# The second FFN's way down: sums of weights made earlier, shared sums kept in PSUM, splits of tokens moved to one engine

## The chip, the cores and the metric

The kernel runs on one core of one Trainium2 chip. The metric is the device time of one launch in microseconds (us); the number given is the median of three runs.

## The reference

One inference step of a backbone with one layer: a half-step FFN, a token mixer (latent attention beside a two-way gated recurrence), a second half-step FFN, a last norm. The change touches the second FFN alone. There are 1152 tokens (1024 latent, 128 context), 1024 model columns and 2816 hidden columns.

```python
def swiglu(h, w1, w3, w2):
    return (jax.nn.silu(h @ w1) * (h @ w3)) @ w2

def trunk_layer(x, mod, cache, lb, norm_g, ffn1, ffn2, mixer_w):
    m = [mod[:, i][:, None, :] for i in range(N_MOD)]
    x = x + 0.5 * m[2] * swiglu(modulate(x, norm_g[0], m[0], m[1]), *ffn1)
    mix, ctx = token_mixer(modulate(x, norm_g[1], m[3], m[4]), cache, lb, *mixer_w)
    x = x + m[5] * mix
    x = x + 0.5 * m[8] * swiglu(modulate(x, norm_g[2], m[6], m[7]), *ffn2)
    return x, ctx
```

## The kernel before

Everything is float32. A float32 product is made of three matmuls, high by high, high by low and low by high, where ScalarE copies the high part of an operand (`wh`, `hh`, `xh`) and VectorE or GpSimd (POOL) subtracts it from the operand for the low part (`wl`, `hl`, `xl`). The names `fp`, `wp` and `dp` are pools of small tiles, of weight tiles and of DRAM. The tokens stand in four quarters of 288 columns; `PAIRS` puts them into two pairs of quarters.

The hidden columns are 22 tiles of 128. **The way up** (`h @ w1`, `h @ w3`) makes tiles 0 to 2 plainly (`plain_block`), and 3 to 21 by seven half products in place of eight, after Strassen and Winograd (`fast_block`, in the order `PRODUCTS = (1, 6, 7, 5, 2, 4, 3)`). Such products need sums of weights: `fast_ops` makes them, on POOL at L1716, their high part on ScalarE at L1720 and their low part on VectorE at L1721. The finished tile goes to DRAM (`hs`); from two tiles, `pair_sums` makes seven sums of tokens and stores them (`xd`).

**The way down** (`@ w2`) takes tiles 3 to 18 in eight pairs, which make three groups: `GROUPS = (3, 2), (7, 3), (13, 3)` holds the first tile of a group and its number of pairs. This is `down_fast`. A group has four sweeps (`down_sweep`), for m = 0 to 3, which stand for output tiles m and m + 4. A sweep runs the seven products, each for both pairs of quarters, so that a sweep of a three-pair group has 7 x 2 x 9 = 126 matmuls of 128x288.

`down_ops` makes the weights of a unit (one group and one m): four loads of w2 quarters (a11, a21, a22, a12), four POOL sums at L1826 (s1 = a21 + a22, s2 = s1 - a11, a11 - a21, a12 - s2), and for each product the high part at L1830 and the low part at L1831. `down_xs` loads the tokens' sums (`xr`, L1844) and splits them (L1854 on ScalarE, L1855 on POOL, or on VectorE for the second pair of a group); those of the next group are made in the third and fourth sweep of a group.

VectorE evicts each product from its PSUM bank (`d`) into the residual stream `x`, times the gate, by `add` at L1871. Products 1 and 6 feed several outputs: their sums over the groups stay in SBUF tiles `S` (named `su`, L1889). In the last group each finished shared sum gives three more adds, the "folds" (`x<-su`); from the second sweep on one fold is run behind each product, and what is left runs beside the first plain tiles.

After the groups, the plain tiles follow: `down_group` for f = 0 and 1 (matmuls at L473 to L475, eviction at L502), then `down_last` for 2, 19, 20 and 21. Their tokens are loaded (`load_h`) and split (`split_h`, L2021 and L2022 for f = 0 and 1 in two halves, one on VectorE and one on POOL) in the last sweep, and their weights by `load_w` (POOL at L247).

A scheduler sets the order of each engine's instructions from the order of the program's lines and their readiness, and pools of tiles decide when a tile may be filled again: three tiles of 384 columns in "hf", two in "raw", eight in the wide pool. All DMAs are put out by SP, in one order.

Of the kernel before, what the change touches and what calls it, by code (L numbers as in the profile page):

```python
# [9 lines left out]
F32 = mybir.dt.float32  # L10
# [4 lines left out]
ALU = mybir.AluOpType  # L15
# [78 lines left out]
class Trunk:  # L94
# [1696 lines left out]

    def down_ops(self, w2):

        nc = self.nc
        units = [(f, n, m) for f, n in GROUPS for m in range(KT // 2)]
        raws = [None, None]

        def load(u, i):
            f, n, m = units[u]
            if i:  # L1800
                t = self.wide("wr")[:, :1024].rearrange("p (v c) -> p v c", v=2)
            else:
                t = self.wp.tile([P, 2, 512], F32, tag="raw", bufs=2, name="raw")
            raws[i] = t[:, :, : n * P]
            for v, (j, h) in enumerate((((0, 0), (1, 0)), ((1, 1), (0, 1)))[i]):
                src = w2[f : f + 2 * n].rearrange("(k h) p o d -> h p k (o d)", h=2)[h]
                nc.sync.dma_start(raws[i][:, v].rearrange("p (k d) -> p k d", k=n), src[:, :, ts(4 * j + m, P)])

        load(0, 0)
        load(0, 1)  # L1810
        c = 0
        for u, (f, n, m) in enumerate(units):
            (a11, a21), (a22, a12) = [(t[:, 0], t[:, 1]) for t in raws]
# [4 lines left out]
            src = {1: a11, 6: s2, 7: a21, 5: s1, 2: a12, 4: a22, 3: a12}  # L1818
            pre = {
                6: ((s1, a21, a22, ALU.add), (s2, s1, a11, ALU.subtract)),  # L1820
                7: ((a21, a11, a21, ALU.subtract),),
                3: ((a12, a12, s2, ALU.subtract),),
            }
            for i in PRODUCTS:
                for o, x, y, op in pre.get(i, ()):
                    nc.gpsimd.tensor_tensor(o, x, y, op)  # L1826
                t = self.wp.tile([P, 2, 512], F32R, tag=("wh", "wl")[c % 2], bufs=3, name="wd")
                wh, wl = t[:, 0, : n * P], t[:, 1, : n * P]
                c += 1
                nc.scalar.copy(wh, src[i])  # L1830
                nc.vector.tensor_sub(wl, src[i], wh)  # L1831
                yield [w.rearrange("p (k d) -> p k d", k=n) for w in (wh, wl)]
# [28 lines left out]
    def down_sweep(self, g, m, X, ops, made, gm, S, after):  # L1861
# [11 lines left out]
        for i in PRODUCTS:  # L1873
            wh, wl = made.pop(0)
            for r, (q0, q1) in enumerate(PAIRS):
# [29 lines left out]
    def down_fast(self, w2, X, xg, ops, made, load_h, split_h, gm, nxt):  # L1905
# [5 lines left out]
        for g, (f, n) in enumerate(GROUPS):  # L1911
            new = {} if g else X
            last = g == len(GROUPS) - 1
            for m in range(KT // 2):
# [6 lines left out]
                def after():  # L1921
# [33 lines left out]
    def ffn_fast(self, l, gm, nxt):  # L1955
# [59 lines left out]
        def split_h(f, raw):  # L2015
            new = partial(self.tt, F32R) if f in (16, 17) and not l else split
            hh, hl = new(name="hh")[:, :T], new(name="hl")[:, :T]
            if isinstance(raw, list):
                for v in range(2):
                    c = ts(v, 2 * QW)  # L2020
                    nc.scalar.copy(hh[:, c], raw[v])  # L2021
                    (nc.gpsimd if v else nc.vector).tensor_sub(hl[:, c], raw[v], hh[:, c])  # L2022
# [7 lines left out]

        dops, dmade, X = (self.down_ops(w2) if l else None), [], {}
        xg = self.down_xs(0, X) if l else None
        for f in range(plain, NF):
# [3 lines left out]
            for n in range(7):  # L2037
# [178 lines left out]
```

## Time and profile before

| what | us |
|---|---|
| median of three runs | 2887.63 (2882.78 to 2887.94) |
| profiled execution, its own time | 2883.36 |
| its span in the profile | 2881.6 |
| TensorE (PE) busy | 2780.9 |
| VectorE (DVE) busy | 2038.8 |
| ScalarE (ACT) busy | 1327.9 |
| POOL busy | 948.6 |

The second FFN's plain tiles of the way up stand at about 2085 to 2150 us of the span, its fast tiles from there to about 2600, the three groups of the way down from about 2590 to 2781, and the plain tiles of the way down after that. PE is the engine of matmuls; PEld, its weight loads, runs beside it. A matmul count in a window is how much was done in it. A row of the timeline gives the start, the time, the engine, the line, the operation, and in brackets the idle time before it with what ended it.

### The profile page before, as it was taken

The page shows a single profiled execution, that of the slowest core. Times are in us where ns is not written, and L with a number is a line of the kernel's source. Part 1 is how long each engine was busy: PE and PEld are TensorE (multiplying, and loading weights), DVE is VectorE, ACT ScalarE, POOL GpSimd, SP SyncE. Part 2 cuts the span into 40 slices and gives each one's busy share as a digit, 9 for nine tenths or more (in the row PEclk, how much of TensorE's full clock was granted, in tenths as well). Part 3 has the DMA queues.
Part 4 walks back from the last instruction along what each step waited for, and adds up shares of the span by engine and source line. Part 5 has one row for each costly group of instructions (what it writes and reads, how often), then busy time and mean ns, then how long its engine had stood idle before and what let it go on. Part 6 is the DMA issues. An engine that isn't in the chain of part 4 may idle for free.

```text
span 2881.6 us, 55237 instructions
## 1 busy us (share of the span) xinstructions
PE 2780.9 (97%) x21138; PEld 2642.9 (92%) x21138; DVE 2038.8 (71%) x4435; ACT 1327.9 (46%) x2714; POOL 948.6 (33%) x947
## 2 busy tenths in 40 slices
PE   6999999999999999999999999989999999999998
PEld 5999999999999998988998777679999999999997
DVE  7677777577778777877355777755766665569885
ACT  6432323321166676766535787731642322334322
POOL 0132233354222122222144444442432222236540
PEclk9999999999999999999999999999999999999999
DMA  6643343653121111112512001263543333256321
GB/s 237 207 144 128 125 124 117 221 209 111 63 81 55 50 57 37 57 47 70 173 52 75 18 16 30 77 218 101 177 138 103 107 118 102 81 177 215 110 83 66
DMA packets 189801, 315.15 MB, mean 109 GB/s; under 512 B 21408, under 2 KB 113632, under 8 KB 189536
## 3 DMA queue, kind: packets, MB, share of 16 engines
q1 hardware_dynamic: 189536, 311.61, 33.2%
q8 instruction: 167, 2.74, 0.4%
q14 instruction: 98, 0.80, 0.1%
HBM read 234.38 MB, written 77.15 MB: 108 GB/s over the span
## 4 chain that ended last, share of the span: by engine, by line
PE 44%; DVE 12%; ACT 7%; issue 3%; DMA 3%; POOL 1%; SPq 0%; DVEq 0%; ACTq 0%; POOLq 0%
PE b L1746 14%; PE d L1884 4%; PE mm L473 4%; PE mm L474 3%; PE mm L475 3%; DMA g<-sgates 2%; PE dn L473 1%; PE dn L475 1%; PE dn L474 1%; PE mps L1411 1%; PE sps L1452 1%; PE lv L960 1%; DVE KE L997 1%; PE sps L1453 1%; PE sps L1454 1%
## 5 line engine op out<-in xcount | busy, mean ns | idle before, releaser
L1746 PE MATMUL b<-xo,wo 128*128 128x288 f32 x3552 | 482.0, 295 | 0.0
L1746 PEld LDWEIGHTS b<-xo,wo 128*128 128x128 f32 x3552 | 474.3, 188 | 0.0
L1746 PE MATMUL b<-bh,wo 128*128 128x288 f32 x1776 | 365.0, 295 | 1.9 <-ACT et L1756 1.9
L473 PE MATMUL mm<-xh,wh 128*128 128x384 f32 (+1 forms) x1008 | 352.5, 350 | 10.7 <-DVE sg L750 5.6
L474 PE MATMUL mm<-xl,wh 128*128 128x384 f32 (+1 forms) x1008 | 342.3, 340 | 0.0
L475 PE MATMUL mm<-xh,wl 128*128 128x384 f32 (+1 forms) x1008 | 341.7, 339 | 0.0
L1746 PEld LDWEIGHTS b<-bh,wo 128*128 128x128 f32 x1776 | 288.6, 188 | 2.1 <-ACT et L1756 2.1
L502 DVE SCALAR_TENSOR_TENSOR x<-dn,modt,x 128x256 f32<-128x256 f32 (+4 forms) x472 | 225.6, 499 | 87.0 <-PE dn L475 85.9
L1746 PE MATMUL b<-bl,wo 128*128 128x288 f32 x888 | 261.4, 294 | 0.0
L1720 ACT CAST wo<-raw 128x512 fp32r<-128x512 f32 x185 | 114.8, 622 | 220.5 <-issue 95.4
L473 PEld LDWEIGHTS mm<-xh,wh 128*128 128x128 f32 (+1 forms) x1008 | 189.8, 188 | 20.7 <-DVE sg L750 7.4
L474 PEld LDWEIGHTS mm<-xl,wh 128*128 128x128 f32 (+1 forms) x1008 | 189.7, 188 | 2.3 <-issue 0.7
L475 PEld LDWEIGHTS mm<-xh,wl 128*128 128x128 f32 (+1 forms) x1008 | 189.4, 188 | 1.0
L1884 PE MATMUL d<-xd,wd 128*128 128x288 f32 x1344 | 183.2, 299 | 6.6 <-DVE x L1871 4.7
L1884 PEld LDWEIGHTS d<-xd,wd 128*128 128x128 f32 x1344 | 181.6, 191 | 8.2 <-ACT wd L1830 4.2
L1721 DVE TENSOR_TENSOR wo<-raw,wo 128x512 fp32r<-128x512 f32 x185 | 127.4, 689 | 77.6 <-ACT wo L1720 75.8
L1716 POOL TENSOR_TENSOR ws<-raw 128x256 f32<-128x256 f32 x74 | 63.1, 873 | 328.5 <-DMA raw<-in_w 293.1
L318 DVE SCALAR_TENSOR_TENSOR junk<-wada,cb 128x512 bf16<-128x512 f32 x224 | 163.1, 728 | 9.7 <-DMA wada<-in_w_aT 8.9
L1461 POOL TENSOR_TENSOR ehl<-e,ehl 128x512 fp32r<-128x512 f32 x93 | 121.7, 1313 | 140.8 <-ACT ehl L1459 79.6
L1746 PEld LDWEIGHTS b<-bl,wo 128*128 128x128 f32 x888 | 167.0, 188 | 0.0
L247 POOL TENSOR_TENSOR wl<-raw,wh 128x1024 fp32r<-128x1024 f32 (+3 forms) x51 | 101.4, 1988 | 174.4 <-ACT wh L246 157.2
L1716 POOL TENSOR_TENSOR raw<-raw,ws 128x256 f32<-128x256 f32 x74 | 55.3, 768 | 285.1 <-issue 278.7
(433 smaller groups left out, 7175.3 us busy)
## 6 DMA issues: line engine op xcount, KB each, us to landing
raw<-in_w SPq DMA_DIRECT2D x148, 256.0 KB, 3.4
wada<-in_w_aT SPq DMA_DIRECT2D x112, 256.0 KB, 3.1
raw<-in_w SPq DMA_DIRECT2D x42, 512.0 KB, 3.9
raw<-in_w_in SPq DMA_DIRECT2D x41, 512.0 KB, 3.4
xr<-xd SPq DMA_DIRECT2D x56, 288.0 KB, 3.7
hr<-hs SPq DMA_DIRECT2D x26, 576.0 KB, 6.0
hb<-hd SPq DMA_DIRECT2D x44, 288.0 KB, 3.3
hs<-et SPq DMA_DIRECT2D x84, 144.0 KB, 2.0
```

What stands on the lines that cost most here:

```text
L247: pin((eng or self.nc.gpsimd).tensor_sub(wl, raw, wh))
L318: nc.vector.scalar_tensor_tensor(junk, ws[n % 2], 1.0, cs[s], ALU.mult, ALU.mult, accum_out=o)
L473: pin(nc.tensor.matmul(ps, wh, xh, start=start and i == 0, stop=False))
L474: pin(nc.tensor.matmul(ps, wh, xl, start=False, stop=False))
L475: pin(nc.tensor.matmul(ps, wl, xh, start=False, stop=stop and i == n - 1))
L502: nc.vector.scalar_tensor_tensor(self.x[m][:, a:b], ps[:, a - lo : b - lo], self.modt[:, gm, m, s : s + 1], self.x[m][:, a:b], ALU.mult, A ...
L1461: eng.tensor_sub(el, e, eh)
L1716: nc.gpsimd.tensor_tensor(o[:, c], x[:, c], y[:, c], op)
L1720: nc.scalar.copy(wh, src[i])
L1721: nc.vector.tensor_sub(wl, src[i], wh)
L1746: nc.tensor.matmul(ps, w[:, k], x[:, k, :QW], start=first, stop=last, skip_group_check=home != i)
L1884: nc.tensor.matmul(ps, w[:, k], xv, start=start, stop=stop, skip_group_check=home != i)
```

## The change

A new generator, `pair_weights`, goes through the five pairs of the first two groups and the four m, 20 units in all. Each unit loads four 128x128 pieces of w2 into two tiles of the "hf" pool (L1802 and L1804 of the changed kernel), makes the four sums on POOL (L1807 to L1810), and stores the results to DRAM (`wsum`, L1812 and L1813). It has four steps a unit, and the fast blocks of the way up take one step behind every product but the fourth. `down_ops` then loads seven ready operands for a unit of the first two groups: those of products 1, 5 and 3 into "hf" tiles (`wq`, L1840), of 6 and 7 into a "raw" tile, of 2 and 4 into a wide tile; the units of the last group load four operands and make their sums on POOL as before (L1878).

In the last group the shared sum of product 6 is written back into its PSUM bank (L1944), and the folds read it from there; they run behind products 7, 5, 2, 4 and 3 of each of the four sweeps (1, 2, 1, 1 and 1 of them), so none is left after the last. In the last sweep the tokens of the first two plain tiles are loaded and split one product sooner or so, and both halves of a split are on POOL (L2075).

```diff
+    def pair_weights(self, w2):
+        nc = self.nc
+        self.wsum = self.dp.tile([sum(n for _, n in GROUPS[:-1]), P, KT // 2, 4, P], F32, name="wsum")
+        for j in range(sum(n for _, n in GROUPS[:-1])):
+            f = GROUPS[0][0] + 2 * j
+            for m in range(KT // 2):
+                a, b = [self.fp.tile([P, CW], F32, tag="hf", bufs=self.hfb, name="wq") for _ in range(2)]
+                (a11, a21, s1), (s2, a12, a22) = [[t[:, ts(i, P)] for i in range(3)] for t in (a, b)]
+                for v, o in enumerate((a11, a21)):
+                    nc.sync.dma_start(o, w2[f][:, 0, ts(4 * v + m, P)])
+                for v, o in enumerate((a12, a22)):
+                    nc.sync.dma_start(o, w2[f + 1][:, 0, ts(4 * v + m, P)])
+                yield
+                yield
+                nc.gpsimd.tensor_tensor(s1, a21, a22, ALU.add)
+                nc.gpsimd.tensor_tensor(s2, s1, a11, ALU.subtract)
+                nc.gpsimd.tensor_tensor(a21, a11, a21, ALU.subtract)
+                nc.gpsimd.tensor_tensor(a12, a12, s2, ALU.subtract)
+                yield
+                nc.sync.dma_start(self.wsum[j][:, m, 0:2], a[:, P:].rearrange("p (k d) -> p k d", k=2))
+                nc.sync.dma_start(self.wsum[j][:, m, 2:4], b[:, : 2 * P].rearrange("p (k d) -> p k d", k=2))
+                yield
...
     def down_ops(self, w2):
...
-            if u + 1 < len(units):
-                load(u + 1, 0)
-                load(u + 1, 1)
-            s1, s2 = [self.fp.tile([P, CW], F32, tag="hf", bufs=self.hfb, name="ws")[:, : n * P] for _ in range(2)]
...
+        units = [(j, n, m) for j, n in enumerate(n for _, n in GROUPS) for m in range(KT // 2)]
+        nxt = {}
+        def rows_of(f, n, h, c):
+            return w2[f : f + 2 * n].rearrange("(k h) p o d -> h p k (o d)", h=2)[h][:, :, ts(c, P)]
+        def load(u, key):
+            if u == len(units):
+                return
+            g, n, m = units[u]
+            j, f = sum(v for _, v in GROUPS[:g]), GROUPS[g][0]
+            own = g == len(GROUPS) - 1
+            part = lambda t, h: t[:, : h * n * P].rearrange("p (h k d) -> p h k d", h=h, k=n)
+            if key in (1, 5, 3):
+                if own:
+                    return
+                t = part(self.fp.tile([P, CW], F32, tag="hf", bufs=self.hfb, name="wq"), 1)[:, 0]
+                if key == 1:
+                    src = rows_of(f, n, 0, m)
+                else:
+                    src = self.wsum[j : j + n][:, :, m, {5: 1, 3: 3}[key]].rearrange("k p d -> p k d")
+                nc.sync.dma_start(t, src)
+                nxt[u, key] = t
+            elif key == 6:
+                t = part(self.wp.tile([P, 1024], F32, tag="raw", bufs=2, name="raw"), 2)
+                for v, kind in enumerate((2, 0)):
+                    src = rows_of(f, n, 0, 4 * v + m)
+                    if not own:
+                        src = self.wsum[j : j + n][:, :, m, kind].rearrange("k p d -> p k d")
+                    nc.sync.dma_start(t[:, v], src)
+                nxt[u, 6], nxt[u, 7] = t[:, 0], t[:, 1]
             else:
+                t = part(self.wide("wr"), 2)
+                for v in range(2):
+                    nc.sync.dma_start(t[:, v], rows_of(f, n, 1, 4 * v + m))
+                nxt[u, 2], nxt[u, 4] = t[:, 0], t[:, 1]
+        for key in (1, 6, 5, 2, 3):
+            load(0, key)
+        for u, (g, n, m) in enumerate(units):
+            load(u + 1, 6)
+            load(u + 1, 2)
+            if g == len(GROUPS) - 1:
+                a11, a21, a12, a22 = [nxt[u, i] for i in (6, 7, 2, 4)]
+                s1, s2 = [
+                    self.fp.tile([P, CW], F32, tag="hf", bufs=self.hfb, name="ws").rearrange("p (k d) -> p k d", k=n)
+                    for _ in range(2)
+                ]
+                pre = {
+                    6: ((s1, a21, a22, ALU.add), (s2, s1, a11, ALU.subtract)),
+                    7: ((a21, a11, a21, ALU.subtract),),
+                    3: ((a12, a12, s2, ALU.subtract),),
+                }
+                nxt.update({(u, 1): a11, (u, 6): s2, (u, 5): s1, (u, 3): a12})
+            else:
+                pre = {}
             for i in PRODUCTS:
...
+                src = nxt.pop((u, i))
+                wh, wl = [t[:, v, : n * P].rearrange("p (k d) -> p k d", k=n) for v in range(2)]
+                nc.scalar.copy(wh, src)
+                nc.vector.tensor_sub(wl, src, wh)
+                if i in (1, 5, 3):
+                    load(u + 1, i)
+                yield wh, wl
...
                 if i == 1 and first:
                     nc.scalar.copy(u, ps)
                 elif i in (1, 6):
-                    nc.vector.tensor_add(u, ps, u)
+                    nc.vector.tensor_add(ps if i == 6 and last else u, ps, u)
                     if i == 6 and last:
-                        self.folds += [partial(add, mi, q, u) for mi, q in ((m + 4, q1), (m + 4, q0), (m, q1))]
+                        self.folds += [partial(add, mi, q, ps) for mi, q in ((m + 4, q1), (m + 4, q0), (m, q1))]
                 elif i in (7, 5):
                     add(m + 4, q1, ps)
                 elif i == 2:
...
                         for _ in range(GROUPS[g + 1][1]):
                             next(xg, None)
                     elif last:
-                        if m:
+                        for _ in range((0, 0, 1, 2, 1, 1, 1)[k]):
                             self.folds.pop(0)()
                         if m == KT // 2 - 1:
-                            if k in (0, 3):
-                                raws.append(load_h(k // 3))
-                            elif k in (2, 4):
+                            if k in (0, 2):
+                                raws.append(load_h(k // 2))
+                            if k in (1, 3):
                                 pend.append(split_h(*raws.pop(0)))
-                            if k in (1, 5):
-                                ws.append(self.load_w(w2[k // 4], 1, D, home=partial(self.tt, F32R)))
+                            if k in (0, 2):
+                                ws.append(self.load_w(w2[k // 2], 1, D, home=partial(self.tt, F32R)))
                     elif not g and not m:
                         next(xg, None)
                     k += 1
...
         for f in rest[:2]:
             pend.append(split_h(*load_h(f)))
         fs, hs = zip(*pend[:2])
-        self.bg = (f() for f in self.folds)
+        assert not self.folds
         self.down_group(w2, fs, hs, gm, ws)
-        for _ in self.bg:
-            pass
         for f in rest[2:]:
             pend.append(split_h(*load_h(f)))
         fs, hs = zip(*pend[2:])
...
                 for v in range(2):
                     c = ts(v, 2 * QW)
                     nc.scalar.copy(hh[:, c], raw[v])
-                    (nc.gpsimd if v else nc.vector).tensor_sub(hl[:, c], raw[v], hh[:, c])
+                    nc.gpsimd.tensor_sub(hl[:, c], raw[v], hh[:, c])
                 return f, (hh, hl)
             nc.scalar.copy(hh, raw)
             nc.gpsimd.tensor_sub(hl, raw, hh)
...
         def load_w2(f):
             return self.load_w(w2[f], 1, D, home=spare if f % 2 else None)
 
+        sums = self.pair_weights(w2) if l else iter(())
         dops, dmade, X = (self.down_ops(w2) if l else None), [], {}
         xg = self.down_xs(0, X) if l else None
         for f in range(plain, NF):
...
                     g.send(w)
                     if n in ((1, 4) if l else (0, 1, 2, 4)):
                         next(ada, None)
+                if n != 3:
+                    next(sums, None)
                 if f == NF - 1 and l:
                     if n:
                         dmade.append(next(dops))
...
                     elif n == 5:
                         ws.append(load_w2(1))
                         self.x = [load_x(0), load_x(1)]
-        assert next(ada, 1) == 1
+        assert next(ada, 1) == 1 and next(sums, 1) == 1
         for t in self.puts:
             self.put(*t)
         if not l:
```

On POOL, in the plain tiles of the way up: `wl` is the low part of a weight of tile f = 1 or 2, `bl` the low part of tokens, whose matmuls follow. Before:

```order
L247 TENSOR_TENSOR wl_24499<-raw_24496,wh_24498 128x1024
L424 TENSOR_TENSOR bl_23433<-xn_24259,bh_23432 128x288
L424 TENSOR_TENSOR bl_23433<-xn_24278,bh_23432 128x288
L424 TENSOR_TENSOR bl_23433<-xn_24298,bh_23432 128x288
L424 TENSOR_TENSOR bl_23433<-xn_24317,bh_23432 128x288
L424 TENSOR_TENSOR bl_23435<-xn_24337,bh_23434 128x288
L424 TENSOR_TENSOR bl_23435<-xn_24356,bh_23434 128x288
```

The same place after the change, where `wq` are the two tiles of a unit of `pair_weights`:

```order
L247 TENSOR_TENSOR wl_24499<-raw_24496,wh_24498 128x1024
L1807 TENSOR_TENSOR wq_25172<-wq_25172,wq_25173 128x128
L1808 TENSOR_TENSOR wq_25173<-wq_25172 128x128
L1809 TENSOR_TENSOR wq_25172<-wq_25172 128x128
L1810 TENSOR_TENSOR wq_25173<-wq_25173 128x128
L424 TENSOR_TENSOR bl_23433<-xn_24259,bh_23432 128x288
L424 TENSOR_TENSOR bl_23433<-xn_24278,bh_23432 128x288
L424 TENSOR_TENSOR bl_23433<-xn_24298,bh_23432 128x288
L424 TENSOR_TENSOR bl_23433<-xn_24317,bh_23432 128x288
L424 TENSOR_TENSOR bl_23435<-xn_24337,bh_23434 128x288
L1807 TENSOR_TENSOR wq_25364<-wq_25364,wq_25365 128x128
L1808 TENSOR_TENSOR wq_25365<-wq_25364 128x128
```

The first unit's four sums now stand ahead of the subtractions of a token tile, and the second unit's among those of the next.

On SP, at the same place (`in_w13` and `in_w2` are weights in DRAM, `hs1` the finished tile, `hd1` the tokens' stage). Before:

```order
L252 DMA raw_24834<-in_w13 128x1024
L1637 DMA hs1_24209<-sl_24257 128x288
L419 DMA hd1_23440<-xn_24259 128x288
L419 DMA hd1_23440<-xn_24278 128x288
L419 DMA hd1_23440<-xn_24298 128x288
```

After:

```order
L1802 DMA wq_25172<-in_w2 128x128 x2
L1804 DMA wq_25173<-in_w2 128x128 x2
L252 DMA raw_24834<-in_w13 128x1024
L1802 DMA wq_25364<-in_w2 128x128
L1637 DMA hs1_24209<-sl_24257 128x288
L419 DMA hd1_23440<-xn_24259 128x288
L419 DMA hd1_23440<-xn_24278 128x288
L1812 DMA wsum_25171<-wq_25172 128x256
L1813 DMA wsum_25171<-wq_25173 128x256
L1802 DMA wq_25364<-in_w2 128x128
L419 DMA hd1_23440<-xn_24298 128x288
```

The unit's loads stand ahead of a weight load of the way up, and its stores, which follow POOL's sums, ahead of the stores of tokens.

On VectorE, in the last sweep of the last group (`d` are PSUM banks, `x` the residual stream, `modt` the gate, `su` a shared sum in SBUF). Before:

```order
L1871 SCALAR_TENSOR_TENSOR x7_29908<-d7_32040,modt_92,x7_29908 128x288
L1871 SCALAR_TENSOR_TENSOR x7_29908<-d7_32051,modt_92,x7_29908 128x288
L1871 SCALAR_TENSOR_TENSOR x7_29908<-d5_32069,modt_92,x7_29908 128x288
L1871 SCALAR_TENSOR_TENSOR x7_29908<-su_29912,modt_92,x7_29908 128x288
L1871 SCALAR_TENSOR_TENSOR x7_29908<-d5_32080,modt_92,x7_29908 128x288
L1871 SCALAR_TENSOR_TENSOR x7_29908<-su_29913,modt_92,x7_29908 128x288
L1871 SCALAR_TENSOR_TENSOR x3_29906<-d1_31980,modt_92,x3_29906 128x160
```

After:

```order
L1944 TENSOR_TENSOR d6_32261<-d6_32261,su_30158 128x288
L1944 TENSOR_TENSOR d6_32272<-d6_32272,su_30159 128x288
L1926 SCALAR_TENSOR_TENSOR x7_30154<-d7_32289,modt_92,x7_30154 128x288
L1926 SCALAR_TENSOR_TENSOR x7_30154<-d6_32261,modt_92,x7_30154 128x288
L1926 SCALAR_TENSOR_TENSOR x7_30154<-d6_32261,modt_92,x7_30154 128x160
L1926 SCALAR_TENSOR_TENSOR x7_30154<-d7_32300,modt_92,x7_30154 128x288
L1926 SCALAR_TENSOR_TENSOR x7_30154<-d6_32261,modt_92,x7_30154 128x128
L1926 SCALAR_TENSOR_TENSOR x3_30152<-d6_32261,modt_92,x3_30152 128x288
```

The shared sum is written into the bank `d6`, and the folds that read `su` before read that bank now, sooner behind product 6.

More of the change, by code (lines that the diff above doesn't have):

```diff
@@ L1792, in down_ops @@
     def down_ops(self, w2):
         nc = self.nc
[L1795 to L1801, printed above, removed]
-            else:
[L1803 to L1807, printed above, removed]
@@ L1809, in down_ops @@
-        load(0, 0)
-        load(0, 1)
-        c = 0
-        for u, (f, n, m) in enumerate(units):
-            (a11, a21), (a22, a12) = [(t[:, 0], t[:, 1]) for t in raws]
-            if u + 1 < len(units):
-                load(u + 1, 0)
-                load(u + 1, 1)
-            s1, s2 = [self.fp.tile([P, CW], F32, tag="hf", bufs=self.hfb, name="ws")[:, : n * P] for _ in range(2)]
[L1818 to L1823, printed above, removed]
+        units = [(j, n, m) for j, n in enumerate(n for _, n in GROUPS) for m in range(KT // 2)]
@@ L1826, in down_ops @@
                     nc.gpsimd.tensor_tensor(o, x, y, op)
+                src = nxt.pop((u, i))
                 t = self.wp.tile([P, 2, 512], F32R, tag=("wh", "wl")[c % 2], bufs=3, name="wd")
-                wh, wl = t[:, 0, : n * P], t[:, 1, : n * P]
+                wh, wl = [t[:, v, : n * P].rearrange("p (k d) -> p k d", k=n) for v in range(2)]
                 c += 1
-                nc.scalar.copy(wh, src[i])
-                nc.vector.tensor_sub(wl, src[i], wh)
-                yield [w.rearrange("p (k d) -> p k d", k=n) for w in (wh, wl)]
+                nc.scalar.copy(wh, src)
[3 more added lines that the diff above has]
+                yield wh, wl
     def down_xs(self, g, X):
```

## The prediction

> **What bounds the kernel now.** I read the page's head and chain first.
>
> ```profile
> span 2881.6 us, 55237 instructions
> PE 2780.9 (97%) x21138; PEld 2642.9 (92%) x21138; DVE 2038.8 (71%) x4435; ACT 1327.9 (46%) x2714; POOL 948.6 (33%) x947
> PE 44%; DVE 12%; ACT 7%; issue 3%; DMA 3%; POOL 1%; SPq 0%; DVEq 0%; ACTq 0%; POOLq 0%
> ```
>
> TensorE is busy 97% of the span and holds most of the chain. The change leaves the number of matmuls as it is, so it can only win what TensorE loses in stalls or at a lower clock, or add such losses. Where these are in the second FFN is seen by counting matmuls in the windows: length, PE busy (count), PEld, DVE, ACT, POOL, granted clock, DMA share, GB/s.
>
> ```profile
> 2105.00:2110.00 5.00, 3.63 (x16) 2.70 (x15) 3.68 (x9) 4.77 (x12) 2.91 (x4) 0.82 0.38 132
> 2140.00:2145.00 5.00, 2.98 (x23) 2.75 (x22) 5.00 (x8) 1.50 (x3) 3.75 (x5) 1.00 0.43 122
> 2200.00:2300.00 100.00, 100.00 (x759) 100.00 (x758) 68.18 (x145) 30.44 (x60) 29.34 (x37) 1.00 0.36 119
> 2620.00:2630.00 10.00, 8.76 (x66) 8.53 (x65) 9.48 (x20) 3.62 (x9) 5.63 (x6) 1.00 0.47 141
> 2630.00:2640.00 10.00, 7.93 (x57) 7.32 (x55) 9.24 (x15) 8.14 (x16) 7.87 (x6) 1.00 0.42 120
> 2640.00:2650.00 10.00, 9.34 (x59) 9.37 (x60) 9.28 (x16) 3.77 (x7) 10.00 (x7) 0.83 0.75 217
> 2660.00:2670.00 10.00, 10.00 (x78) 10.00 (x77) 7.47 (x14) 2.06 (x4) 2.21 (x3) 1.00 0.16 42
> 2710.00:2720.00 10.00, 9.05 (x67) 8.61 (x65) 7.97 (x11) 5.35 (x9) 10.00 (x7) 1.00 0.86 255
> 2720.00:2730.00 10.00, 8.34 (x51) 8.37 (x52) 9.96 (x19) 2.78 (x6) 6.24 (x5) 0.83 0.46 139
> 2780.00:2790.00 10.00, 5.15 (x23) 4.13 (x21) 9.89 (x8) 5.48 (x6) 10.00 (x5) 0.87 0.16 53
> 2790.00:2800.00 10.00, 9.43 (x45) 9.33 (x45) 5.57 (x13) 0.01 (x1) 4.71 (x2) 0.79 0.01 2
> 2800.00:2810.00 10.00, 10.00 (x59) 10.00 (x58) 6.46 (x14) 0.00 (x0) 0.00 (x0) 1.00 0.00 0
> ```
>
> An undisturbed stretch of the way down has 78 matmuls in 10 us (2660), one of plain tiles 59 (2800). The way up (2200 to 2300) never stops. So the losses stand at four joints:
>
> - J1, first to second group (2620 to 2650): 66 + 57 + 59 = 182 of 234; 52 missing at 7.8 per us are 6.7 us.
> - J2, second to last group (2710 to 2730): 118 of 156, 4.9 us.
> - J3, last group to the plain tiles (2780 to 2800): 23 + 45 = 68 of 118; 50 at 5.9 per us are 8.5 us.
> - J0, the plain tiles of the way up (2105, 2140): short stalls while VectorE prepares the tokens' sums.
>
> J1 to J3 together are 20.1 us, which is all that can be won there. Next, what ends the waits, from the timeline (start, us, engine, line, then idle time and its releaser).
>
> ```profile
> 2622.91 11.15 PEld L1884 LDWEIGHTS d<-xd,wd 128*128 128x128 f32 x84 [1.47 <-DVE x L1871]
> 2720.56 0.51 ACT L1830 CAST wd<-wr 128x384 fp32r<-128x384 f32 x1 [1.27 <-POOL wr L1826]
> 2721.63 13.49 PEld L1884 LDWEIGHTS d<-xd,wd 128*128 128x128 f32 x90 [2.07 <-ACT wd L1830]
> ...
> 2766.90 3.18 POOL L2022 TENSOR_TENSOR hl<-hr,hh 128x576 fp32r<-128x576 f32 x2 [2.91 <-ACT hh L2021]
> 2770.04 2.91 POOL L247 TENSOR_TENSOR wxl<-raw,wxh 128x1024 fp32r<-128x1024 f32 x1
> 2778.06 3.97 DVE L1871 SCALAR_TENSOR_TENSOR x<-su,modt,x 128x160 f32<-128x160 f32 x2
> 2784.21 2.83 POOL L2025 TENSOR_TENSOR hl<-hr,hh 128x1152 fp32r<-128x1152 f32 x1
> 2784.49 0.51 DVE L1871 SCALAR_TENSOR_TENSOR x<-d,modt,x 128x288 f32<-128x288 f32 x1
> 2785.03 2.32 DVE L1871 SCALAR_TENSOR_TENSOR x<-su,modt,x 128x288 f32<-128x288 f32 x1
> 2787.84 0.29 PEld L473 LDWEIGHTS dn<-hh,wxh 128*128 128x128 f32 x1 [4.34 <-DVE x L1871]
> ```
>
> J1 waits for VectorE's evictions, J2 for a weight sum of POOL, and J3 4.34 us for VectorE, whose adds of shared sums from SBUF (su) take 2 to 2.3 us each while POOL runs its long subtractions. The eviction from PSUM (d) at 2784.49, beside the same POOL instruction, takes 0.51.
>
> **J3: shared sums from PSUM, splits on POOL.** Durations by shape:
>
> ```profile
> L1871 DVE SCALAR_TENSOR_TENSOR x<-d,modt,x 128x288 f32<-128x288 f32 x96 | 47.0, 507 | 5.8 <-PE d L1884 5.4
> L1871 DVE SCALAR_TENSOR_TENSOR x<-su,modt,x 128x288 f32<-128x288 f32 x20 | 19.6, 979 | 0.4
> ```
>
> After the change all of these adds read PSUM (d6 in the order): 0.51 us instead of a mean of 0.98, and not 2 or more beside POOL. VectorE also gives up two halves of the first plain tiles' splits. None of the folds is left after the last sweep. VectorE should then be a product behind at 2781, not 6 us. POOL gains two halves of 3.18 / 2 = 1.6 us; its work of this stretch has idle time around it (2.91 before the first half), and by the row at 2770.04 its last weight split ended at 2773, so with 3.2 more it ends near 2776, ahead of the first plain matmuls at about 2781. The banks of product 6 now stay taken until their folds are done: the second pair's is written again 27 matmuls into the next sweep, 3.5 us at 7.8 per us, against folds of 0.5. In the first sweep of the last group six folds stand where none stood (+3 us of VectorE); that goes to J2. J3's bounds: 4 (only the 4.34 us wait goes, the half clock behind it stays) to 8.5. I take **−7.5**, near the upper end, because nothing of what VectorE does there still reads two SBUF operands.
>
> **J1 and J2: ready sums are loaded.** POOL loses four sums for each of the eight units of the first two groups:
>
> ```profile
> L1826 POOL TENSOR_TENSOR wr<-wr,ws 128x256 f32<-128x256 f32 x4 | 3.0, 741 | 11.4 <-DVE wd L1831 11.4
> L1826 POOL TENSOR_TENSOR ws<-raw,wr 128x256 f32<-128x256 f32 x4 | 4.0, 1008 | 0.0
> L1826 POOL TENSOR_TENSOR ws<-raw,wr 128x384 f32<-128x384 f32 x8 | 8.6, 1078 | 24.7 <-DMA wr<-in_w 22.7 <-issue 1.9
> L1826 POOL TENSOR_TENSOR raw<-raw 128x384 f32<-128x384 f32 x8 | 9.6, 1201 | 0.5
> ```
>
> That is 16 × 0.74 to 1.01 and 16 × 1.08 to 1.20, about 32 us less. At J1 POOL was busy up to 10.00 of 10 and VectorE 9.3; POOL gets room, and VectorE's subtractions run beside it less often. Against this stand seven loads a unit where four were, all in SP's one row; the three into the small ring are put out only after VectorE's low part (L1831) of the product before has freed their tile, and the token loads (xr) stand behind them. A load lands in some 3.6 us:
>
> ```profile
> wr<-in_w SPq DMA_DIRECT2D x8, 128.0 KB, 3.6
> ```
>
> One unit's lead covers that (126 matmuls of a three-pair unit are 16 us). J1's bounds: +2 (the new loads hold the xr loads for half a landing) to −6.7; I take **−3.5**, half the loss, since VectorE's evictions, which ended the wait, keep their own number and length. J2 waits for a sum of the last group's own unit, which stays on POOL and in the same place, but gets a less loaded POOL ahead of it and six more folds on VectorE: between +2.5 and −4.9, I take **−0.5**.
>
> [...]
>
> **J0 and the way up: the sums' new place.** POOL gets 80 adds of 128x128. The trace has none; between 0.40 (128x48) and the 0.74 above, by columns, 0.53 each, 2.1 a unit, 42 us in all.
>
> ```profile
> L907 POOL TENSOR_TENSOR Y<-fs,Y 128x48 f32<-128x48 f32 x72 | 28.5, 396 | 109.1 <-ACT Y L905 105.5
> 2097.43 1.57 POOL L424 TENSOR_TENSOR bl<-xn,bh 128x288 fp32r<-128x288 f32 x2 [0.35 <-ACT bh L423]
> PEld ps L474 <- POOL bl L424: 1.9, 4, 0.6
> 2115.10 5.46 DVE L1633 TENSOR_TENSOR xo<-hd,xo 128x288 fp32r<-128x288 f32 x4
> 2127.97 1.56 DVE L1633 TENSOR_TENSOR xo<-hd,xo 128x288 fp32r<-128x288 f32 x4
> ```
>
> On 42 us of an engine that is 29% busy in the way up, the average is harmless. But the order puts the first units into the plain tiles: the first four adds stand ahead of the bl subtractions at 2097, for which TensorE waits already, and the next four among them. One unit on that path is +2.1. VectorE's four subtractions took 5.46 us beside 4.8 us of POOL and 1.56 alone: 0.8 us lost for each us of POOL. Where VectorE is full (5.00 of 5 at 2140) another unit's 2.1 us thus cost 1.7. J0: **+3.8**, from 0 (the adds fall into POOL's idle time) to 6 (all three units on the path).
>
> [...]
>
> In the fast blocks the weights stand ready early:
>
> ```profile
> 2316.88 1.25 DVE L1721 TENSOR_TENSOR wo<-ws,wo 128x512 fp32r<-128x512 f32 x1 [3.05 <-ACT wo L1720]
> 2329.23 0.46 DVE L1750 TENSOR_TENSOR et<-b,et 128x288 f32<-128x288 f32 x1
> POOL ws L1716 <- DMA raw<-in_w: 159.1, 17, 11.7
> ```
>
> This low part is there at 2318.1, and its product, 12 matmuls ahead of its first eviction, starts at about 2327.6: 9.5 us of cover, against 2.1 of adds in front of a sum. I take **+0.5** (0 to 21, see below). If the cover were gone, each unit would cost its 2.1.
>
> **Sum.** −7.5 − 3.5 − 0.5 + 3.8 + 0.5 = −7.2. The profiled execution took 2883.36 us, 4.27 below the median of the runs (2887.63): 2876.2 on its scale, **2880.4** against the median. About 0.2%, 5.8 us, is what a measurement of this kernel can tell from no change: faster means below 2881.9, slower above 2893.4.
>
> **Rivals.**
>
> - *The loads take the sums' place* (chance 0.14). J1 and J2 keep their losses because TensorE waits for loads that SP holds back where it waited for VectorE and POOL. For: SP is in order, and the DMA share at J1 is 0.75 already. Against: the stretches have gaps at 0.42 to 0.47. −7.5 + 3.8 + 0.5 = −3.2, 2884.4.
> - *Slower: the way up is coupled to the pair sums* (0.16). SP holds a store of sums until POOL has made them; POOL makes them behind its own weight sums, which wait for raw loads (17 waits, 159.1 us), and those stand behind the store on SP. From the point where a raw load comes 9.5 us later than now, TensorE stops in the middle of a tile. Such a stop is taken at 3 us (1.5 idle, as at 2622.91, and 1.7 at the clock of 0.83 over 10 us). 80 steps, six a tile, run over 13 tiles; in half of them, 7 × 3 = 21: +13.8, 2901.4. For: the waits are up to 11.7 us already. Against: TensorE doesn't stop once from 2200 to 2300.
> - *J1 and J2 vanish and J0 is free* (0.10). −7.5 − 6.7 − 4.9 are −19.1, 2868.5. For: POOL's 10.00 of 10 at both joints. Against: VectorE's evictions remain.
> - *J3 doesn't go as said* (0.06): TensorE then waits for POOL, which now has all of the splits. Only 3 of 8.5 won: −2.7, 2884.9. For: POOL is 10.00 busy from 2780; against: its margin of 5 us above.
> [...]
>
> **How the numbers follow.** The forecast has 0.50. Of it 0.40 lie below 2881.9, since the J0 and J1 terms can each be off by 3; 0.10 within. Faster: 0.40 + 0.10 + 0.02 = 0.52. Within 0.2%: 0.10 + 0.12 + 0.05 + 0.02 = 0.29. Slower: 0.16 and the tails of the first and fourth rival, 0.03, are 0.19. The range begins at the third rival, 2868, and ends at 2895, where the forecast's costs all stand at their bad ends (−4 + 2 + 2.5 + 6 + 0.5 = +7); only the second rival lies outside.
>
> **What would show it.** Right: at J3 over 100 matmuls in the two windows, the folds at 0.5 us and no wait for VectorE above 1 us; at J1 POOL well below 10.00 and 25 matmuls more; in the plain tiles TensorE waits for bl by 2 us more; 2200 to 2300 with 759 matmuls still. Wrong: stops in the fast blocks released by wo or by raw loads, J3's wait handed to POOL's hl, or J0 longer by over 6 us.

## The result

The changed kernel takes 2880.3 us (median of 22 runs), the kernel before 2884.45 us in the 22 runs beside them: a ratio of 0.9985, 95% interval 0.9979 to 0.9992, so some 2 to 6 us less, 4.3 by the ratio. Forecast were 7.2 less, which lies outside this interval. The time itself, 2880.4 forecast and 2880.3 measured, agrees better than the difference only because the kernel before took 2884.45 us here and not the 2887.63 from which the forecast reckons; that is luck. The profiled executions have spans of 2881.6 and 2876.7 us.

The windows of the changed kernel (length, PE busy with its count, PEld, DVE, ACT, POOL, granted clock, DMA share, GB/s), at the four joints and in the way up:

```profile
2105.00:2110.00 5.00, 3.18 (x16) 2.27 (x16) 3.17 (x8) 4.49 (x11) 3.99 (x7) 1.00 0.67 218
2200.00:2300.00 100.00, 100.00 (x759) 100.00 (x758) 68.32 (x144) 28.12 (x60) 42.81 (x62) 1.00 0.47 151
2620.00:2630.00 10.00, 9.63 (x73) 9.38 (x72) 7.64 (x20) 3.48 (x8) 2.99 (x2) 1.00 0.83 262
2630.00:2640.00 10.00, 7.92 (x59) 7.55 (x58) 6.62 (x12) 6.95 (x14) 4.92 (x4) 1.00 0.66 197
2640.00:2650.00 10.00, 6.21 (x36) 6.00 (x35) 10.00 (x14) 4.81 (x9) 8.76 (x5) 0.83 0.79 233
2710.00:2720.00 10.00, 10.00 (x78) 10.00 (x77) 8.99 (x13) 5.39 (x9) 10.00 (x7) 1.00 0.81 254
2720.00:2730.00 10.00, 7.73 (x57) 7.32 (x56) 8.57 (x16) 4.61 (x9) 7.09 (x6) 1.00 0.69 207
2730.00:2740.00 10.00, 9.40 (x71) 9.17 (x70) 9.83 (x25) 2.06 (x4) 4.27 (x4) 1.00 0.19 52
2780.00:2790.00 10.00, 10.00 (x67) 10.00 (x66) 6.45 (x15) 5.36 (x6) 10.00 (x5) 1.00 0.47 165
2790.00:2800.00 10.00, 10.00 (x60) 10.00 (x59) 6.10 (x14) 1.53 (x2) 8.31 (x4) 1.00 0.01 2
```

J3 is gone: TensorE is busy 10.00 of 10 in both of its windows where it was 5.15 and 9.43, the whole 8.5 us. J1 is longer: 73 + 59 + 36 = 168 of 234 matmuls, 8.5 us lost in place of 6.7. J2, shifted, has 78 + 57 + 71 = 206 of 234, 3.6 us in place of 4.9 (and three matmuls, 0.4 us, are missing at 2750 to 2760). The way up has its 759 matmuls as before. For J0 one window holds all plain tiles, first of the kernel before:

```profile
2080.00:2160.00 80.00, 76.14 (x537) 74.24 (x536) 52.53 (x103) 44.26 (x96) 31.75 (x27) 0.96 0.46 145
```

and of the changed kernel:

```profile
2080.00:2160.00 80.00, 73.27 (x523) 70.94 (x522) 53.94 (x102) 44.89 (x96) 38.45 (x39) 0.98 0.50 160
```

14 matmuls at the 7.4 per us of these tiles (222 in 30 us) are 1.9 us. Together -8.5 + 1.8 - 1.3 + 0.4 + 1.9 = -5.7, against -4.9 between the spans.

The two windows of J0 differ in the granted clock, however, 0.96 and 0.98, and it is the kernel before that was slowed more. Two of the experiments below leave this part as it was before and have 0.98 too, with 550 and 551 matmuls; the second (folds from PSUM, old splits):

```profile
2080.00:2160.00 80.00, 76.19 (x551) 74.47 (x549) 54.61 (x108) 44.79 (x97) 31.78 (x27) 0.98 0.48 151
```

Against these the changed kernel lacks 27 or 28 matmuls, 3.6 to 3.8 us. So J0 costs 1.9 us between the two profiles and about 3.7 at a like clock; how often the clock falls there in the timed runs isn't known.

What TensorE waits longer for at J0 is in the groups of waits of 2100 to 2160 (what waited, for what: us in all, times, longest). The kernel before:

```profile
PEld ps L473 <- DVE sl L1676: 2.2, 1, 2.2
PEld ps L474 <- POOL bl L424: 1.9, 4, 0.6
```

The changed kernel:

```profile
PEld ps L473 <- DVE sl L1676: 3.9, 2, 2.4
PEld ps L474 <- POOL bl L424: 3.7, 5, 1.7
```

The wait for POOL's `bl` is 1.8 us longer (one unit's sums, forecast 2.1), the wait for VectorE 1.7 (forecast 1.7).

At J1 the waits of 2618 to 2652 in the kernel before read

```profile
ACT xd L1854 <- DMA xr<-xd: 9.4, 6, 3.5
POOL xd L1855 <- ACT xd L1854: 5.6, 2, 3.6
PEld d L1884 <- ACT wd L1830: 2.1, 1, 2.1
```

and in the changed kernel

```profile
POOL xd L1910 <- ACT xd L1909: 15.6, 3, 8.9
ACT xd L1909 <- DMA xr<-xd: 10.9, 8, 3.2
PE d L1939 <- DVE x L1926: 6.2, 3, 3.8
PEld d L1939 <- ACT xd L1909: 4.0, 1, 4.0
```

POOL has got its room and stands idle in it: it waits 8.9 us at a stretch for the cast of the next tokens, then has eight subtractions to do in a row while TensorE waits 4.00 us for those tokens.

SP's own waits of 2610 to 2645 show which loads hold its row. The kernel before:

```profile
SPq L1844 <- POOL xd L1855: 14.8, 8, 4.5
SPq L1807 <- DVE wd L1831: 3.7, 2, 2.3
```

The changed kernel:

```profile
SPq L1848 <- DVE wd L1884: 4.6, 2, 3.2
SPq L1840 <- DVE wd L1884: 3.1, 1, 3.1
```

Over all such groups, SP waits 3.9 us at weight loads before (L1807) and 10.4 after (L1848, L1840), mostly for VectorE to free their tiles, and the token loads stand behind them; at the token loads themselves it waits 21.9 us before (L1844) and 10.0 after (L1899).

### The profile page after: what moved, and what is told of

Read it like the earlier page. It is cut to its first block, busy times and chain, and to the rows that moved or that the text cites. A ratio compares the mean times of both kernels' runs of the same rounds, so it can differ in the third digit from the quotient of the medians.

```text
span 2876.7 us, 55574 instructions
## 1 busy us (share of the span) xinstructions
PE 2780.8 (97%) x21138; PEld 2642.9 (92%) x21138; DVE 2023.5 (70%) x4433; ACT 1324.6 (46%) x2714; POOL 962.9 (33%) x997
## 5 line engine op out<-in xcount | busy, mean ns | idle before, releaser
L1721 DVE TENSOR_TENSOR wo<-ws,wo 128x512 fp32r<-128x512 f32 x74 | 71.6, 967 | 112.4 <-ACT wo L1720 112.2
L1720 ACT CAST wo<-ws 128x512 fp32r<-128x512 f32 x74 | 45.6, 617 | 223.2 <-POOL ws L1716 223.1
```

## The experiments

Each was timed in five rounds against the kernel before on the same chip, so the ratios compare them and not the medians. The ratios in one table, then each by itself:

| kernel | median us | ratio to before, 95% |
|---|---|---|
| changed kernel | 2880.3 | 0.9985 (0.9979 to 0.9992) |
| folds and splits alone | 2876.32 | 0.9974 (0.9965 to 0.9983) |
| pair sums alone | 2886.6 | 1.0007 (0.9998 to 1.0016) |
| changed, pair sums two tiles later | 2873.94 | 0.9968 (0.9956 to 0.9981) |
| changed, token loads first | 2879.22 | 0.9985 (0.9977 to 0.9994) |
| folds sooner, from SBUF, with the splits | 2877.58 | 0.9975 (0.9965 to 0.9985) |
| splits alone | 2886.46 | 1.0009 (1.0000 to 1.0018) |
| folds sooner, from PSUM, old splits | 2877.5 | 0.9977 (0.9969 to 0.9986) |
| sums later, early tokens | 2875.55 | 0.9968 (0.9956 to 0.9981) |
| folds and splits, early tokens | 2876.82 | 0.9972 (0.9963 to 0.9982) |
| sums later, 16 token loads left out | 2871.32 | 0.9958 (0.9946 to 0.9969) |
| sums later, tokens on ScalarE's queue | 2875.75 | 0.9970 (0.9958 to 0.9982) |
| sums later, 60 more POOL sums | 2899.27 | 1.0051 (1.0039 to 1.0063) |

### The two halves of the change

Folds and splits alone: `pair_weights` and its steps taken out, `down_ops` as before.

> The last group's part alone (shared sums in PSUM, splits sooner and on POOL), weights' sums as in the kernel before. Theory 'the joints add': the whole gain of the change is the joint behind the last group, 8.5 us by the matmul counts of the two traces, and the pair sums cost the rest (J0 +2.4, J1 +1.8, J2 -0.9), so this kernel is about 8.5 us faster than before (ratio 0.9970), 4 us faster than the changed one; J1 keeps 182 matmuls in 2620 to 2650, the plain tiles keep 16 in 2105 to 2110 and 23 in 2140 to 2145, and 2780 to 2800 has about 127. Rival 'POOL must be relieved first': without the pair sums POOL (10.00 busy at the last joint) is late with the splits and at the second joint; then the gain is only 3 to 5 us (0.9983 to 0.9990) and TensorE waits for hl.

Pair sums alone: `down_sweep`, `down_fast` and `split_h` as before.

> The pair sums alone (made in the way up, loaded for the first two groups), the last group's folds and splits as in the kernel before. 'The joints add': slower than before by 2.4 + 1.8 - 0.9 = 3.3 us (ratio 1.0011), with the last joint still at about 68 matmuls of 118. Rival: the pair sums help the joint between the second and the last group by more than the count says (the folds in the first sweep of the last group took it back in the changed kernel): then J2's loss falls to 1 or 2 us and the kernel is level with before or up to 2 us faster.

The joints add. The first half by itself is worth 0.26%, 7.5 us; the second costs 0.07%, 2 us, in an interval that just holds no change. POOL didn't have to be relieved first.

### Sums out of the plain tiles

```diff
-                if n != 3:
+                if n != 3 and f > plain + 1:
                     next(sums, None)
```

> The changed kernel with the pair sums' steps begun two fast tiles later, so that none of them stands among the plain tiles. If the hoisted sums are what costs J0 2.4 us, the windows 2080 to 2160 go back to 545 matmuls and the time is 2.4 us below the changed kernel's, 6.5 to 7 us below before (ratio 0.9977). Rival: J0's difference is something else (the order of SP's loads or chance): then it stays at 527 and the ratio at 0.9985.

The waits of 2100 to 2160 are back where they were, and the window 2080 to 2160 has 541 matmuls, 18 more than the changed kernel (2.4 us; the expectation's 545 and 527 are sums of shorter windows, which count a matmul at an edge twice):

```profile
PEld ps L473 <- DVE sl L1676: 2.3, 1, 2.3
PEld ps L474 <- POOL bl L424: 1.8, 4, 0.6
```

J0's cost was the place of the sums, as forecast. The ratio fell by more than these 2.4 us: 0.9985 to 0.9968 are 4.9, and the spans differ by 5.0. J1 has 77 + 33 + 67 = 177 of 234 here, 7.3 us lost for 8.5. Of the remaining 1.4 us most isn't due to the sums: ahead of 2050 us, where the two kernels are alike, this profile is 9 matmuls further (15348 for 15339), more than 1 us. The two intervals touch. No kernel of this study that computes all of the reference has a lower ratio; two of those below have 0.9968 and 0.9970.

### What J3 needed

Folds run sooner, but from SBUF as before:

```diff
-                    nc.vector.tensor_add(ps if i == 6 and last else u, ps, u)
+                    nc.vector.tensor_add(u, ps, u)
...
-                        self.folds += [partial(add, mi, q, ps) for ...]
+                        self.folds += [partial(add, mi, q, u) for ...]
```

> As the kernel with the last group's part alone (8.5 us faster than before), but the shared sum of product 6 goes to its SBUF tile as before; the folds run at the same sooner places and read it there. 'PSUM is what counts' (as predicted: folds from SBUF take 1 us, and 2 to 4 us beside POOL's subtractions): the folds' mean is again about 1 us, VectorE is late at 2781 and half or more of the 8.5 us is lost (ratio 0.9985 or above). Rival 'the place is what counts': what cost J3 was three folds left over for the plain tiles; run sooner they do no harm from SBUF either, and the ratio stays at 0.9974 to 0.9978.

The splits alone, put into the kernel before:

> The kernel before with only the splits and loads of the first two plain tiles moved (sooner, both halves on POOL), folds as before. VectorE is relieved of two halves (about 1 us each, more beside POOL) but the folds from SBUF still stand against more work of POOL. 'PSUM counts': J3 gains 0 to 2 us (ratio 0.9993 to 1.0000). Rival 'the splits on VectorE were the brake': 4 us or more (0.9986 or below).

And the folds alone, from PSUM, with the old splits:

> The kernel before with the folds from PSUM, run sooner, and the splits of the first plain tiles left as they were (later, one half on VectorE). Splits alone gave nothing, folds sooner from SBUF with the new splits gave the whole 7 us. If the folds' place is all that counts, this gives 0.9973 to 0.9978 too; if the new splits are needed beside it (VectorE's halves in the last sweep put it behind again, or the tokens come late), the ratio is 0.9983 or above and TensorE waits at the first plain tiles for hl or x.

This is the miss of the mechanism. Folds from SBUF at the sooner places win 0.25%, as much as from PSUM (0.26% with the new splits, 0.23% with the old); the new splits by themselves win nothing. Folds from SBUF at the sooner places were run with the new splits only. VectorE's groups of 2700 to 2800 in the kernel with sooner folds from SBUF, and its windows:

```profile
L1871 DVE SCALAR_TENSOR_TENSOR x<-d,modt,x 128x288 f32<-128x288 f32 x40 | 19.6, 507 | 2.1 <-PE d L1884 2.0
L1871 DVE SCALAR_TENSOR_TENSOR x<-su,modt,x 128x288 f32<-128x288 f32 x20 | 15.4, 768 | 0.3
```

```profile
2780.00:2790.00 10.00, 9.57 (x60) 9.29 (x60) 8.82 (x18) 6.44 (x6) 10.00 (x5) 1.00 0.35 119
2790.00:2800.00 10.00, 10.00 (x59) 10.00 (x58) 6.32 (x13) 0.00 (x0) 8.34 (x4) 1.00 0.01 2
```

A fold from SBUF still takes 0.77 us for 0.51, and VectorE is 8.82 busy after 2780 where the changed kernel has 6.45. But none is left over: TensorE loses 0.43 us at J3, and its 60 + 59 = 119 matmuls are 4 fewer than the 64 + 59 with folds from PSUM and the same splits. So PSUM is worth some 0.7 us of the 8.5 here. In the splits-only kernel, with folds where they were, the last adds from SBUF stand behind the last sweep again, beside POOL's long subtractions (its timeline):

```profile
2777.91 5.07 DVE L1871 SCALAR_TENSOR_TENSOR x<-su,modt,x 128x160 f32<-128x160 f32 x2
2782.89 0.51 DVE L1871 SCALAR_TENSOR_TENSOR x<-d,modt,x 128x288 f32<-128x288 f32 x1
2783.44 2.36 DVE L1871 SCALAR_TENSOR_TENSOR x<-su,modt,x 128x288 f32<-128x288 f32 x1
```

### What holds J1

The token loads moved up in SP's order by a small priority around their issue:

> The changed kernel with the loads of the tokens' sums (xr) moved up in SP's order by a small priority, so that two or three of them pass the weight loads (raw<-wsum) that hold SP at J1. 'SP holds the tokens back': POOL's idle time in 2620 to 2636 (4.5 and 8.9 us waiting for the tokens' cast) shrinks and J1 gets back 2 to 6 us (ratio to before 0.9965 to 0.9978). Rival 'buffers hold the tokens': the xr loads wait for their own tiles, set free by POOL and VectorE, and the order on SP changes nothing: J1 keeps 168 matmuls in 2620 to 2650 and the ratio stays at 0.9985.

In its trace four token loads instead of two are put out from 2620 to 2626, ahead of the next `raw<-wsum`; but from 2633 SP puts out nothing until 2636.5, as in the changed kernel. J1 counts 72 + 53 + 40 = 165 matmuls, 8.8 us lost: nothing gained. The next kernels all have the pair sums two tiles later. Six token tiles made a sweep sooner (with the pair sums, and without them):

> The changed kernel with the pair sums begun two tiles later (as in the run that gave 0.9968) and with six of the 21 token tiles of the second group made already in the third sweep of the first group. If J1 waits because POOL and ScalarE get 21 token tiles at once behind the sweep that frees their places ('tokens late'), J1 loses under 3 us where it lost 7: ratio 0.9950 to 0.9958. Rival 'VectorE's evictions bound J1': POOL is less pressed but TensorE still waits for x; the ratio stays at 0.9965 to 0.9970.

> The last group's part alone, without the pair sums, with the same six token tiles made early. If 'tokens late' holds and the pair sums add nothing to it, the ratio goes from 0.9974 to 0.9958 or below, level with the kernel that has the pair sums and the early tokens; if POOL's weight sums stand in the early tokens' way, it stays above 0.9965 and the pair sums have a worth of their own of 3 us or more.

Neither moved a ratio, and with the pair sums J1 is no shorter by the counts either (71 + 33 + 60 = 164 of 234). The two ratios, 0.9968 and 0.9972, have intervals that overlap, so a worth of the pair sums of their own isn't shown. With the pair sums, POOL's wait in front of its eight subtractions was there again:

```profile
2618.94 2.99 POOL L1910 TENSOR_TENSOR xd<-xr,xd 128x576 fp32r<-128x576 f32 x2 [5.20 <-ACT xd L1909]
2630.88 13.64 POOL L1910 TENSOR_TENSOR xd<-xr,xd 128x576 fp32r<-128x576 f32 x8 [8.95 <-ACT xd L1909]
```

Then the loads of 16 of the 21 token tiles were left out, and, with all of them in, put on ScalarE's queue:

> The changed kernel with the pair sums begun two tiles later, and the second group's token sums loaded for the first 5 of its 21 tiles only; the other 16 tiles are cast and split from those 5 again, so the loads (xr) of 16 tiles are left out and the second group computes with the wrong tokens. 'SP holds the tokens back' (POOL idles 9 to 15 us at J1 for a cast that waits for its load): J1 loses 2 us or less where it lost 7.2 (100 of 156 matmuls in 2630 to 2650), ratio 0.9945 to 0.9955. Rival 'places, casts and evictions hold them' (the wide tiles that the weights w2 of products 2 and 4 share with the tokens of products 7 and 5, VectorE full): J1 still loses 5 us or more, ratio 0.9962 or above.

> As the kernel with the pair sums two tiles later, with the token loads of the second and third groups put out by ScalarE in place of SP, all of them. 'SP holds the tokens back': they pass the weight loads, J1 and J2 lose less, ratio 0.9950 to 0.9960. Against it: ScalarE then itself waits for the tiles that POOL and VectorE set free, and its casts of weights stand behind; if that is the tighter queue, J1 is longer and the ratio is above 0.9968.

Windows of the kernel without the 16 loads:

```profile
2620.00:2630.00 10.00, 8.88 (x67) 8.65 (x67) 9.26 (x21) 3.32 (x9) 2.21 (x2) 1.00 0.35 100
2630.00:2640.00 10.00, 8.25 (x62) 8.04 (x62) 10.00 (x17) 9.94 (x19) 8.79 (x6) 1.00 0.27 79
2640.00:2650.00 10.00, 10.00 (x78) 10.00 (x77) 10.00 (x17) 2.53 (x5) 6.89 (x4) 1.00 0.59 170
```

Windows with the loads on ScalarE's queue:

```profile
2620.00:2630.00 10.00, 10.00 (x77) 10.00 (x77) 7.91 (x20) 3.12 (x8) 2.30 (x2) 1.00 0.51 143
2630.00:2640.00 10.00, 8.79 (x67) 8.59 (x66) 9.26 (x19) 6.49 (x13) 4.89 (x3) 1.00 0.62 175
2640.00:2650.00 10.00, 10.00 (x77) 10.00 (x77) 10.00 (x16) 6.67 (x13) 8.65 (x6) 1.00 0.66 208
```

Without the loads J1 loses 27 / 7.8 = 3.5 us in place of 7.3. On the other queue it loses 13 / 7.8 = 1.7, but TensorE loses 1.8 us more just ahead of it, at 2590 to 2610 (70 + 68 matmuls for 75 + 77), so that 3.8 us are won in both. Leaving the loads out also takes their traffic away; the other queue keeps it (DMA share 0.51 to 0.66) and wins as much, which speaks for the place in SP's row and against the traffic. So about half of J1 is the lateness of the token loads on SP; that is shown by the counts, while the time (0.9958 against 0.9968) agrees without setting the two apart. Neither run came out as expected: 3.5 us and 0.9958 lie between the two cases of the first, and on the other queue J1 got shorter but the ratio, 0.9970, did not fall. Its J2 has 71 + 60 + 62 = 193 of 234 for the 201 of the kernel it is compared with, which takes 1 us of the gain back.

What makes the other half isn't settled: without the loads VectorE is 9.26 to 10.00 busy in all three windows, which fits its evictions, but no run took work from it there. Nor were the token loads moved in a kernel without the pair sums, so it isn't known how much of the 6.7 us that J1 cost before is the same lateness.

### How much the way up can take

The first of each unit's four sums made four times:

> As the kernel with the pair sums two tiles later, with the first of each unit's four sums made four times over, so 20 x 3 = 60 more POOL adds of 128x128 in the way up (about 32 us of POOL). If the way up hides POOL's adds as forecast (cover 9.5 us), the fast blocks keep 759 matmuls per 100 us and the ratio stays at 0.9968 within its interval. Rival 'the cover is nearly gone': stops between 2160 and 2580, slower than that kernel by 5 us or more.

The rival holds, and the forecast's cover doesn't. 60 more sums of about 0.6 us, 36 us of POOL, cost 24 us by the two ratios (1.0051 and 0.9968), and 164 matmuls (3178 to 3014), 21.6 us at 7.59 per us, are missing between 2160 and 2580. One stop in its timeline:

```profile
2438.81 2.41 POOL L1808 TENSOR_TENSOR wq<-wq 128x128 f32<-128x128 f32 x4 [1.97 <-issue]
...
2447.30 1.43 POOL L1716 TENSOR_TENSOR ws<-raw 128x256 f32<-128x256 f32 x2 [4.71 <-DMA raw<-in_w]
...
2450.16 0.62 ACT L1720 CAST wo<-ws 128x512 fp32r<-128x512 f32 x1 [11.45 <-POOL ws L1716]
2450.81 1.24 DVE L1721 TENSOR_TENSOR wo<-ws,wo 128x512 fp32r<-128x512 f32 x1 [9.26 <-ACT wo L1720]
...
2451.97 0.81 DVE L1754 TENSOR_TENSOR et<-b,et 128x288 f32<-128x288 f32 x2
2452.05 0.70 ACT L1756 ACTIVATE et<-b 128x288 f32<-128x288 f32 x2
2452.56 0.37 PE L1746 MATMUL b<-bh,wo 128*128 128x288 f32 x1 [2.00 <-ACT et L1756]
```

TensorE doesn't wait for the late weight. VectorE stands 9.26 us at the subtraction that makes the weight's low part, ScalarE 11.45 us at its high part, and the evictions of PSUM banks that stand behind these in their queues come late: TensorE waits for a bank. All waits of its matmuls between 2160 and 2600, seven in all, are for `et`:

```profile
PE b L1746 <- ACT et L1756: 12.1, 5, 3.7
PE b L1746 <- DVE et L1752: 2.3, 1, 2.3
PE b L1746 <- DVE et L1754: 1.4, 1, 1.4
```

The weight is late because its load is. SP stands 5.1 us at the store of the unit's sums (L1813) until POOL has made them, and the load of the weight, `raw`, comes behind the two stores:

```profile
2442.20 0.33 SPq L1813 DMA_DIRECT2D wsum<-wq  x1
2442.63 1.29 SPq L1814 DMA_DIRECT2D wsum<-wq  x1
2444.01 10.20 SPq L1698 DMA_DIRECT2D raw<-in_w  x4
```

It lands at 2447.3, where POOL goes on after 4.71 us. From 2160 to 2600 SP waits 70.8 us for the sums at the first of the two stores (20 waits), and 31.3 (13 waits) in the changed kernel with its four sums a unit. This is the coupling that the prediction's second rival names.

## Why the prediction was right, and where it was not

- **J3, -7.5**: measured -8.5 by the matmuls; the half alone gave -7.5 in time. The size was right, the reason wrong. The step that failed is "near the upper end, because nothing of what VectorE does there still reads two SBUF operands". It can read them; what counts is that the folds run in the sweep that makes them, and also in the first one, so that none is left for the end; PSUM added some 0.7 us. The folds from SBUF were slow beside POOL's subtractions: in the kernel before four of 128x288 took 2.08 to 2.75 us while POOL worked (2772 to 2790), and 0.52 the one at 2776.09, which began while POOL stood idle; with the splits alone the fold at 2783.44 took 2.36 us and the eviction from PSUM at 2782.89, beside the same POOL work, 0.51. But the end didn't hang on it. The half clock in the forecast's bounds is 0.50 in the kernel before from 2788 to 2794 us, 0.87 and 0.79 over the two windows; the changed kernel has 1.00 in both.
- **J1, -3.5**: measured +1.8, near the bad bound of +2, by the mechanism of the first rival. The step that failed is "POOL gets room": room is no gain where the engine's next input isn't there, and POOL waited 8.9 us at a stretch for its own. The kernel before showed the sign already, with 9.4 us of ScalarE's waits at J1 for the loads of tokens. The rival's own reason, loads held on SP, is shown for about half of it. Its second part, that J2 would keep its loss, did not come.
- **J2, -0.5**: measured -1.3 and +0.4 behind it.
- **J0, +3.8**: measured +1.9 between the two profiles, and about 3.7, the forecast, against profiles with the same clock; both mechanisms as forecast, 1.8 and 1.7 us of longer waits. A sum of 128x128 took 0.60 us, not 0.53.
- **The way up, +0.5**: measured 0, but for a wrong reason. The 9.5 us by which a weight is ready weren't the cover; the cover is how long VectorE's and ScalarE's queues may stand before an eviction is late. With seven sums in a unit in place of four, the second rival's stops came, by the way it names: SP held the weight's loads behind the stores of the sums.
- **The chances**: 0.02 of faster and 0.02 of within 0.2% stood for dips of the clock at J1 and J2 that stay whatever the stops do. No run shows that they must: at J1 the changed kernel has 0.83 as before, but the folds and splits alone 1.00; at J2 the changed kernel has 1.00 where 0.83 was.

J1 was off by 5.3 us; J3, J0, J2 and the way up gave 1.0, 1.9, 0.4 and 0.5 back, from -7.2 to -5.7 by the counts, or to -3.9 with 3.7 us for J0; the ratio has -4.3 (-2.3 to -6.1). That the total is off by no more than 3 us is luck: errors of both signs made up for each other.

## What to carry to other kernels

Work that is left over behind a stage may be cured, as here, by doing it inside the stage; try that before moving its operands to another memory. When an engine that was full at a joint is relieved, look up at once what it would do next and whether the input is there, above all where one in-order queue issues both the loads that were added and those that it waits for (here SP stood 10.4 us at weight loads, ahead of the token loads that POOL needed). The cover of a step on a busy in-order engine is not how early its product is ready, but how soon what stands behind it in the queue is missed (here ScalarE stood 11.45 us at one cast and VectorE 9.26 at the subtraction after it, and TensorE waited 2.00 us for an eviction behind them).

## What the runs showed of the hardware

The dip of the granted clock at J1 isn't a fixed price of its stops. The kernel with the folds and splits alone stands still for longer in the window 2640 to 2650, at full clock, where the kernel before shows 0.83:

```profile
2640.00:2650.00 10.00, 8.10 (x62) 7.99 (x61) 10.00 (x15) 4.21 (x7) 10.00 (x7) 1.00 0.72 215
```

TensorE is busy 8.10 here and 9.34 there, with 62 and 59 matmuls. Nor does the dip lengthen J1: from 2620 to 2660 the kernel with the dip has 259 matmuls and the other one 262. It is behind by 14 at 2650 (182 for 196, where 182 were expected of both) and gets 11 of them back by 2660, where the other one stops again (77 for 66). There is one profile of each kernel, so whether the dip comes with the kernel or with the execution was not shown.
